# Third and fourth group's output projection as one of six steps, and an order planned in both directions

## The chip, the cores and the metric

The kernel runs on one core of one Trainium2 chip. The metric is device time in microseconds (us). TensorE is called PE below, VectorE DVE, ScalarE ACT, GpSimd POOL, and SyncE, which issues most DMAs, SP.

## The reference

Two layers are computed, for one prompt of 1024 tokens and 8 samples of 4 tokens, 1056 tokens in all, with 1024 features. Layer 0 is a Hawk block, layer 1 an HGRN2 block; a norm closes the trunk. The change lies in layer 0 and in the first two products of layer 1. Layer 0 is, cut to what matters:

```python
xn = _rmsnorm(x, g_norm)
u = xn @ w_in                                  # 1024 -> 2 x 1536
xb, gate = u[..., :1536], u[..., 1536:]
xc, new_buf = _causal_conv(xb, conv_w, conv_b, buf)      # 4 taps
r  = sigmoid(xc . w_r + b_r)                   # 16 blocks of 96
ig = sigmoid(xc . w_i + b_i)
log_a = -8 * softplus(-lam) * r
a = exp(log_a)
bterm = sqrt(-expm1(2 * log_a)) * (ig * xc)
h[t] = a[t] * h[t-1] + bterm[t]                # along the tokens
y = h * silu(gate)
return x + y @ w_out                           # 1536 -> 1024
```

## The kernel before

Features lie on the partitions, tokens along the free axis, in three chunks (c) of 352 tokens. x has 8 blocks of 128 features (k, or m for outputs); the 1536 inner features are 12 blocks in 4 groups (g) of three (j). A product in fp32 is made of three matmuls of fp32r parts (`mm3`, lines 192 to 194): high weight by high x, high by low, low by high. So every weight and every operand is split into a high part (a copy, on ACT) and a low part (a subtraction, on DVE or POOL; `subtract`, line 360). A projection of x to one block and chunk is 8 steps, 24 matmuls of 352 columns; one of a group's y to one block of x is 3 steps, 9 matmuls.

Layer 0 isn't ordered by hand. Its functions record operations in `fl`, a `Flow` (line 48): engine, an estimated duration, the call, the keys read and written, and a priority. `Flow.run` is a list scheduler: at each step it takes the engine that can start first and, among that engine's ready operations, the one of the lowest priority number, then of the earliest place in the program. The products recorded with `main=True` keep their program order on PE; the small gate products of the recurrence, the norms and the broadcasts are side work that the planner puts between them, made ready later by `SIDE`, 0.8 us. The order found is emitted as it is: each engine has its fixed queue, and an instruction that waits holds up all behind it on its engine. Layer 1 after its first six products is scheduled by the framework.

The program order of layer 0 is as follows. `begin(c, ...)` loads a chunk of x, scales and splits it, sums its squares (`squares`, L456 on ACT, L459 the adds) and takes its norm (`norm`: PE L281 sums over partitions, DVE L471, POOL's power L473, DVE L474 and L477 make a diagonal, PE L479 broadcasts it to a PSUM bank). `scaled_parts` (L484 and L485) multiplies by gain and norm and splits. Chunk 0 is split from the unnormalized x (L844, L847, L850) and its norm is applied to the products (L506, L546). `products(c)` multiplies the first six blocks of weights, group 0's gate and conv columns. `gate(g)` evaluates the gate half of a group, with ACT's tanh and a multiplication on DVE, into `sg`. `conv(g)` evaluates the other half: a 4-tap filter (L522, L525), whose result is split into X, 18 blocks that all groups use in turn (L530, L531). `lru(g)` makes the gates of the recurrence from X (PE, hg banks), rebuilds the filter's result on POOL (L601), scans (L621) and multiplies by the gate's `sg` (L629). `split_y(g)` splits the result into YH and YL (L636, L637). `out(g)` multiplies y by the output weights of the group, 8 blocks by 3 chunks of 9 matmuls, adds to x (L652), which it loads from and stores to DRAM: xT to x1a, x1a to x1b, x1b to x1c for g = 0, 1, 2. `out_last` does the same for g = 3, chunk by chunk with the weights of all eight blocks kept in X (L677, L678), adds (L691), squares on ACT, adds them on POOL, and norms for layer 1. `first1` is the first two weight blocks of layer 1.

The stages after the start stand in this order before the change:

```python
lru(0); split_y(0); gate(1); conv(1); gate(2, (0, 1)); lru(1); out(0)
gate(2, (2,)); split_y(1); conv(2); lru(2); gate(3, (0,)); out(1)
split_y(2); conv(3); gate(3, (1, 2)); lru(3); out(2); split_y(3); out_last
```

Four PSUM banks (`mm`) take the main products in turn, four (`hg`) the side products; a bank is free again when the product's evacuation has read it. Weights pass through three raw buffers (`raws`).

Of the kernel before, what the change touches and what calls it, by code (L numbers as in the profile page):

```python
# [38 lines left out]
CH = 352  # L39
# [7 lines left out]
class Flow:  # L47
# [3 lines left out]
    HOP, SIDE = 0.2, 0.8  # L51
    EARLY = {"PE": 0.0, "DVE": 0.0, "ACT": 0.0, "POOL": 0.0, "SP": 0.0}

    def __init__(self):
        self.ops = []
        self.writer = {}
        self.readers = {}
        self.main = None
        self.dma_free = 0.0
# [23 lines left out]

    def run(self):
        left = [len(o[3]) for o in self.ops]
        after = [[] for _ in self.ops]
        for i, o in enumerate(self.ops):
            for d in o[3]:
                after[d].append(i)
        ready = [0.0] * len(self.ops)  # L90
        wait = {e: [] for e in self.EARLY}
        free = dict(self.EARLY)
        for i, n in enumerate(left):
            if not n:
                wait[self.ops[i][0]].append(i)
        self.log = []
        for _ in self.ops:
            t0, e = min((max(free[e], min(ready[i] for i in q)), e) for e, q in wait.items() if q)
            q = wait[e]
            i = min((j for j in q if ready[j] <= t0), key=lambda j: (self.ops[j][4], j))  # L100
            q.remove(i)
            _, us, emit, _, _, kb, _ = self.ops[i]
            emit()
            end = free[e] = t0 + us
            if kb:
                self.dma_free = max(self.dma_free, t0 + 2.6) + kb / 250.0
                end = self.dma_free
            self.log.append((i, e, t0, end))
            for j in after[i]:
                o = self.ops[j]  # L110
                ready[j] = max(ready[j], end + (self.HOP + o[6] if o[0] != e or kb else 0.0))
                left[j] -= 1
                if not left[j]:
                    wait[o[0]].append(j)
# [12 lines left out]
def tile_trunk(ctx: ExitStack, tc: tile.TileContext, xT, prm, hc, w0, wg, wo0, w1, wo1, s_in,  # L127
# [205 lines left out]
    with ExitStack() as l0:  # L333
# [12 lines left out]
        def dma(dst, src, r=(), w=(), prio=5, kb=180, q=Q):  # L346
            fl.add("SP" if q is Q else "ACT", 0.45, lambda: q.dma_start(dst, src), r, w, prio, kb)
# [7 lines left out]
        def pool(n, emit, r, w, prio=5):  # L355
            fl.add("POOL", 0.3 + 0.0026 * n, emit, r, w, prio)
# [93 lines left out]


        def squares(k, x, xk, acc, eng=None, own=None):
# [3 lines left out]
            act(CH, lambda: S.activation(sq[:, :CH], x, AF.Square), (xk,), (sk,), 2)  # L456
# [81 lines left out]
        def gate(g, js=range(3)):  # L538
# [17 lines left out]
        def lru(g):  # L556
# [11 lines left out]
            for c in range(NCH):  # L568
# [40 lines left out]
                for j in range(3):  # L609
# [9 lines left out]
                    h, hk = ta[:, j], tak[j]  # L619
# [4 lines left out]
                    if c == 2:  # L624
                        pool(1, lambda h=h, m=m: G.tensor_copy(hst[:, m, 0:1], h[:, 319:320]), (hk,), (("hst", m),), 4)
                        pool(8, lambda h=h, m=m: G.tensor_copy(hst[:, m, 1:], h[:, 320:].rearrange("p (b j) -> p b j", j=4)[:, :, 3]),
                             (hk,), (("hst", m, 1),), 4)
                    sg, sk = sgs[g][j, c]
                    dve(CH, lambda h=h, sg=sg: V.scalar_tensor_tensor(sg, h, 0.5, sg, op0=ALU.mult, op1=ALU.mult), (hk, sk), (sk,), 3, True)  # L629

        def split_y(g):
            for c in range(NCH):
                for j in range(3):
                    sg, sk = sgs[g][j, c]
                    a, b = YH[j][:, chunk(c)], YL[j][:, chunk(c)]
                    act(CH, lambda sg=sg, a=a: S.copy(a, sg), (sk,), (("yh", j, c),), 2)  # L636
                    dve(CH, lambda sg=sg, a=a, b=b: V.tensor_tensor(b, sg, a.bitcast(F32), op=ALU.subtract),  # L637
                        (sk, ("yh", j, c)), (("yl", j, c),), 2, True)
# [4 lines left out]
        def out(g, src, dst, more, ms=range(KD)):  # L643

            own = cycle([next(xos) for _ in range(NXO)] + more)
            for m in ms:
# [19 lines left out]
        def out_last(src):  # L666

            ws = []
            for m in range(KD):
                raw, rk = next(raws)  # L670
                dma(raw[:, :384], wo0[m][:, 1152:], (), (rk,), 1, 192)
                keys = []
                for i in range(2):
                    a = (2 * m + i) * 384
                    keys.append(tuple(("X", b) for b in range(a // CH, (a + 383) // CH + 1)))
                hi, lo = (X[:, (2 * m + i) * 384:(2 * m + i + 1) * 384] for i in range(2))
                act(384, lambda hi=hi, raw=raw: S.copy(hi, raw[:, :384]), (rk,), (*keys[0], ("wl", m, 0)), 1)  # L677
                pool(384, lambda hi=hi, lo=lo, raw=raw: G.tensor_tensor(lo, raw[:, :384], hi.bitcast(F32), op=ALU.subtract),  # L678
                     (rk, ("wl", m, 0)), (*keys[1], ("wl", m, 1)), 1)
                ws.append(lambda k, hi=hi, lo=lo, m=m: (hi[:, 128 * k:128 * k + 128], lo[:, 128 * k:128 * k + 128],  # L680
                                                        (("wl", m, 0), ("wl", m, 1))))
            own = [next(xos) for _ in range(NXO)]
            spare = halves[0][:8], own + [halves[0][8]] + [halves[1][i] for i in (0, 3, 6, 1)], halves[0][:8]
            for c in range(NCH):
                acc = next(xbs)
                rows = []
                for m in range(KD):
                    ps, pk = product(ws[m], ycols(c), 1)
                    x, xk = spare[c][m]
                    dma(x, src[m][:, chunk(c)], ((3, m, c),), (xk,), 3)  # L690
                    dve(CH, lambda x=x, ps=ps: V.tensor_tensor(x, ps[:, :CH], x, op=ALU.add), (pk, xk), (xk,), 0)  # L691
                    dma(x1d[m][:, chunk(c)], x, (xk,), (("x1d", m, c),), 3)
                    squares(m, x, xk, acc)
                    rows.append((x, xk))
# [636 lines left out]
```

## Time and profile before

| | us |
|---|---|
| median of 3 runs | 1145.92 |
| lowest and highest | 1145.76, 1146.29 |
| profiled execution, its own time | 1146.4 |
| its span in the profile | 1144.6 |
| PE busy | 1111.9 |
| DVE busy | 683.0 |
| ACT busy | 487.1 |
| POOL busy | 470.0 |

The mean granted clock of PE over the span is 0.986 of full speed. In the profile an instruction is named by its source line (L192), its engine, its operation and its output and inputs by the program's names; `sg`, `xb`, `xo`, `k` and `R` are buffers that serve several purposes, and the line tells which. Windows are counted from the span's start. What an idle stretch is put down to is the operation whose completion released the waiting one. Layer 0 ends near 540 us.

### The profile page before, as it was taken

What the parts mean: (1) busy time and instruction counts of PE and PEld (TensorE: products, weight loads), DVE (VectorE), ACT (ScalarE), POOL (GpSimd) and SP (SyncE); (2) the same over time, 40 slices, a digit from 0 to 9 for tenths busy, and PEclk for the clock granted to TensorE, in tenths of its full rate; (3) what the DMA queues carried; (4) which work ended last, traced back from release to release, by engine and by line L of the source; (5) the groups of instructions that cost most, each with busy time, mean ns of one, the idle gap of its engine ahead of it and who ended that gap; (6) DMA issues with size and microseconds to landing.
All of it is one profiled execution on the core that took longest, in us unless ns stands there. A gap on an engine that the chain in (4) does not pass through costs nothing.

```text
span 1144.6 us, 24338 instructions
## 1 busy us (share of the span) xinstructions
PE 1111.9 (97%) x9688; PEld 1065.8 (93%) x9688; DVE 683.0 (60%) x1373; ACT 487.1 (43%) x1112; POOL 470.0 (41%) x491
## 2 busy tenths in 40 slices
PE   8899999999999999989999999999999999989996
PEld 7799999999999999889999999999999999979995
DVE  6988488686668857983343534443543534486426
ACT  7443767845666585552223132222223232242323
POOL 4622254434344435674143423324143423263444
PEclk9899999999999999999999999999999999999998
DMA  8201122483276238741112111121112111151204
GB/s 274 64 13 37 56 68 67 141 253 95 60 213 209 62 88 260 256 160 38 37 40 77 38 59 39 45 70 38 59 39 77 40 58 39 34 193 38 81 9 152
DMA packets 70977, 105.15 MB, mean 92 GB/s; under 512 B 9296, under 2 KB 51920, under 8 KB 70864
## 3 DMA queue, kind: packets, MB, share of 16 engines
q1 hardware_dynamic: 68704, 100.91, 28.1%
q10 hardware_dynamic: 2160, 2.69, 0.7%
q8 instruction: 76, 1.25, 0.5%
q14 instruction: 37, 0.30, 0.1%
HBM read 72.13 MB, written 26.57 MB: 86 GB/s over the span
## 4 chain that ended last, share of the span: by engine, by line
PE 89%; DVE 7%; ACT 1%; issue 1%; POOL 0%; DMA 0%; POOLq 0%; DVEq 0%; ACTq 0%
PE mm L192 26%; PE mm L194 24%; PE mm L193 24%; PE hg L986 2%; PE hg L1107 1%; PE hg L1065 1%; PE hg L586 1%; PE hg L960 1%; PE hg L1109 1%; PE hg L193 1%; PE hg L194 1%; PE hg L192 1%; DVE xl L360 1%; PE hg L1041 1%; DVE sg L484 1%
## 5 line engine op out<-in xcount | busy, mean ns | idle before, releaser
L192 PE MATMUL mm<-xh,whi 128*128 128x352 f32 x1368 | 458.6, 335 | 0.0
L193 PE MATMUL mm<-xl,whi 128*128 128x352 f32 x1368 | 443.6, 324 | 1.8 <-POOL xl L360 1.8
L194 PE MATMUL mm<-xh,wlo 128*128 128x352 f32 x1368 | 443.9, 324 | 0.1
L192 PEld LDWEIGHTS mm<-xh,whi 128*128 128x128 f32 x1368 | 258.2, 189 | 9.5 <-issue 4.2
L193 PEld LDWEIGHTS mm<-xl,whi 128*128 128x128 f32 x1368 | 258.5, 189 | 4.5 <-POOL xl L360 2.1
L194 PEld LDWEIGHTS mm<-xh,wlo 128*128 128x128 f32 x1368 | 258.0, 189 | 1.7 <-issue 1.2
L171 POOL TENSOR_TENSOR wlo<-wraw,whi 128x512 fp32r<-128x512 f32 x76 | 92.8, 1224 | 216.4 <-ACT whi L170 216.3
L360 POOL TENSOR_TENSOR wlo<-wraw,whi 128x512 fp32r<-128x512 f32 (+1 forms) x65 | 93.9, 1455 | 99.4 <-ACT whi L415 94.0
L525 DVE SCALAR_TENSOR_TENSOR k<-xb,prm_sb,k 128x352 f32<-128x352 f32 (+2 forms) x144 | 88.7, 627 | 8.3 <-ACT k L522 3.8
L170 ACT CAST whi<-wraw 128x512 fp32r<-128x512 f32 x76 | 44.0, 586 | 114.8 <-PE mm L193 95.7
L930 ACT ACTIVATE t<-mm 128x352 f32<-128x352 f32 x66 | 30.5, 461 | 110.2 <-PE mm L194 106.9
L192 PE MATMUL mm<-yh,whi 128*128 128x352 f32 x216 | 71.6, 331 | 0.5 <-DVE xo L652 0.4
L194 PE MATMUL mm<-yh,wlo 128*128 128x352 f32 x216 | 69.8, 323 | 0.0
L193 PE MATMUL mm<-yl,whi 128*128 128x352 f32 x216 | 69.8, 323 | 0.0
L1048 DVE TENSOR_TENSOR AV<-AV,Gc 128x512 f32<-128x512 f32 (+1 forms) x42 | 36.1, 860 | 42.9 <-PE hg L1041 19.7
L1120 POOL TENSOR_TENSOR rst<-rst,mhalf 128x4 f32<-128x4 f32 (+1 forms) x24 | 20.6, 861 | 90.8 <-DVE rst L1119 90.8
L601 POOL TENSOR_TENSOR k<-X 128x352 f32<-128x352 f32 x36 | 38.0, 1057 | 44.7 <-DVE R L602 40.1
L415 ACT CAST whi<-wraw 128x512 fp32r<-128x512 f32 (+1 forms) x67 | 37.3, 579 | 32.6 <-PE mm L193 17.6
L582 ACT ACTIVATE R<-hg,smalls 128x352 f32<-128x352 f32 x72 | 37.8, 553 | 11.8 <-PE hg L194 9.5
L192 PEld LDWEIGHTS mm<-yh,whi 128*128 128x128 f32 x216 | 40.7, 188 | 1.9 <-DVE xo L652 0.7
L193 PEld LDWEIGHTS mm<-yl,whi 128*128 128x128 f32 x216 | 40.7, 189 | 0.6
L945 DVE SCALAR_TENSOR_TENSOR SG<-t,mm 128x352 f32<-128x352 f32 x24 | 12.4, 519 | 48.0 <-ACT t L930 48.0
(315 smaller groups left out, 2114.2 us busy)
## 6 DMA issues: line engine op xcount, KB each, us to landing
wraw<-in_w_dram SPq DMA_DIRECT2D x105, 256.0 KB, 2.7
wraw<-in_wo_dram SPq DMA_DIRECT2D x32, 192.0 KB, 2.6
sg<-in_xT_dram SPq DMA_DIRECT2D x27, 176.0 KB, 3.8
x<-x SPq DMA_DIRECT2D x8, 528.0 KB, 4.3
si<-in_s_in_dram SPq DMA_DIRECT2D x8, 512.0 KB, 3.5
out_ss_out_dram<-si SPq DMA_DIRECT2D x8, 512.0 KB, 2.6
sg<-x1c SPq DMA_DIRECT2D x21, 176.0 KB, 4.0
x<-sg SPq DMA_DIRECT2D x21, 176.0 KB, 2.0
```

What stands on the lines that cost most here:

```text
L170: S.copy(hi, raw[:, :n])
L171: G.tensor_tensor(lo, raw[:, :n], hi.bitcast(F32), op=ALU.subtract)
L192: T.matmul(out, wh, xh, start=first, stop=False)
L193: T.matmul(out, wh, xl, start=False, stop=False)
L194: T.matmul(out, wl, xh, start=False, stop=last)
L360: emit = lambda: e.tensor_tensor(b, x, a.bitcast(F32), op=ALU.subtract)
L415: act(m, lambda hi=hi, raw=raw, m=m: S.copy(hi[:, :m], raw[:, :m]), rk, (hk,), prio)
L525: dve(u, lambda src=src, dst=dst, sh=sh, k=k: V.scalar_tensor_tensor(dst, sh(src, k), pc("cw", 12 * k + m), dst, op0=ALU.mult, op1=ALU.add ...
L582: act(CH, lambda ps=ps, R=R, i=i, j=j, hb=hb, m=m: S.activation(R[:, i, j], ps[:, :CH], AF.Tanh, bias=hb[:, m:m + 1], scale=0.5), (pk, ("s ...
L601: pool(CH, lambda x=x, a=a, b=b: G.tensor_tensor(x, a.bitcast(F32), b.bitcast(F32), op=ALU.add), (ak, bk), (xk,), 3)
L930: S.activation(t, ps[:, :CH], AF.Tanh, scale=0.5)
L1048: V.tensor_tensor(av[:, :, 1, :], av[:, :, 1, :], gv[:, :, 0:1].to_broadcast([128, nb, level]), op=ALU.mult)
```

## The change

The change has these parts.

- `out` serves groups 0 and 1 only. `out_last` multiplies the y of groups 2 and 3 at once: each of its 24 products has six steps, 18 matmuls, and adds to x1b. The loads, adds and stores of x1c go. Group 3's y lies in the places of x's first three blocks (`xcols(c)[:3]`), no longer needed by then. Its weights are 768 columns for each block instead of 384 and are loaded in 18 pieces into the places of the recurrence's gate weights (m = 4), X (m = 0 to 3), the third chunk's places of x blocks 3 to 7 (m = 5 and part of 6) and two weight buffers (the rest of 6, and 7). Blocks are taken in the order 4, 0, 1, 2, 3, 5, 6, 7, in the third chunk 6, 7, 5, 4, 0, 1, 2, 3.
- The last two gate columns of group 3 are multiplied behind the group's recurrence, chunk by chunk (`by_chunk`): the scan writes h into the gate's place, and the gate's evacuation multiplies it (`late`).
- The order of stages differs: conv(2) directly follows group 2's gates, out(0) comes behind lru(2), conv(3) and lru(3) ahead of out(1).
- In the start, chunk 0's low parts are all made on DVE (`XG` is empty), four of its squares on POOL (`MU`), the parameters are the second load of ACT's queue, and the small constants of layer 0 (`smalls`) are computed at the start, apart from layer 1's (`smalls1`).
- `Flow` plans forwards by priorities, then backwards from the end, then forwards with the backward plan's start times as priorities, eight times, and emits the shortest of the plans. `SIDE` is 1.2 us; a load's completion is a delay of its readers only.
- In `first1`, the first weight block's second chunk now comes ahead of the second block's first.

The diff, cut:

```diff
-    HOP, SIDE = 0.2, 0.8
+    HOP, SIDE = 0.2, 1.2
+    TURNS = 8
     def run(self):
+        best = got = self.plan([o[4] for o in self.ops])
+        for _ in range(self.TURNS):
+            got = self.plan(self.back(got[2]))
+            self.ends.append(got[0])
+            best = min(best, got, key=lambda g: g[0])
+        for i in best[3]:
+            self.ops[i][2]()
...
+        def by_chunk(items):
+            ws = [weights(src, 1024) for src, _ in items]
+            for c in range(NCH):
+                for w, (_, evac) in zip(ws, items):
+                    evac(c, *product(w, xcols(c)))
+                    yield
...
+            if mult:
+                pool(CH, lambda: G.tensor_tensor(sq[:, :CH], x, x, op=ALU.mult), (xk,), (sk,), 2)
+            else:
+                act(CH, lambda: S.activation(sq[:, :CH], x, AF.Square), (xk,), (sk,), 2)
...
+                    if late:
+                        t, tk = next(ts)
+                        act(CH, lambda: S.activation(t, ps[:, :CH], AF.Tanh, scale=0.5), (pk,), (tk,), 0)
+                        dve(CH, lambda: V.scalar_tensor_tensor(t, t, 1.0, ps[:, :CH], op0=ALU.add, op1=ALU.mult), (pk, tk), (tk,), 0)
+                        dve(CH, lambda: V.scalar_tensor_tensor(sg, sg, 0.5, t, op0=ALU.mult, op1=ALU.mult), (tk, sk), (sk,), 1, True)
+                        return
...
         def out_last(src):
-            ws = []
-            for m in range(KD):
-                raw, rk = next(raws)
-                dma(raw[:, :384], wo0[m][:, 1152:], (), (rk,), 1, 192)
+            def load(m, k, n, hi, hks, lo, lks, kept=()):
+                raw, rk = next(raws)
+                u = 128 * n
+                a, b = ("wl", m, 0, k), ("wl", m, 1, k)
+                dma(raw[:, :u], wo0[m][:, 768 + 128 * k:768 + 128 * k + u], (), (rk,), 1, u / 2)
+                act(u, lambda: S.copy(hi, raw[:, :u]), (rk,), (*hks, a), 1)
+                pool(u, lambda: G.tensor_tensor(lo, raw[:, :u], hi.bitcast(F32), op=ALU.subtract), (rk, a), (*lks, b), 1)
...
             for c in range(NCH):
-                for m in range(KD):
-                    ps, pk = product(ws[m], ycols(c), 1)
-                    dma(x, src[m][:, chunk(c)], ((3, m, c),), (xk,), 3)
+                for i, m in enumerate(ms[c]):
+                    ps, pk = product(blocks[m].get, ycols(c) + xcols(c)[:3], 1)
+                    dma(x, src[m][:, chunk(c)], ((2, m, c),), (xk,), 3)
...
-        VI, XG = (0, 2), (1, 3, 5)
+        VI, XG, MU = (0, 2), (), [(0, k) for k in range(1, 8, 2)]
...
-        run(project0(gate(2, (0, 1))))
+        gates, rest = project0(gate(2)), out(0, xT, x1a)
+        run(islice(gates, 6))
         lru(1)
-        run(out(0, xT, x1a, halves[0][6:]))
-        run(project0(gate(2, (2,))))
-        split_y(1)
+        run(gates)
         run(project0(conv(2)))
         lru(2)
-        run(project0(gate(3, (0,))))
-        run(out(1, x1a, x1b, halves[1][3:]))
+        run(rest)
+        split_y(1)
+        run(project0(gate(3,(0,))))
+        rest = out(1, x1a, x1b)
+        run(project0(conv(3)))
+        lru(3)
+        run(rest)
+        run(by_chunk(gate(3, (1, 2), True)))
         split_y(2)
-        run(project0(conv(3)))
-        run(project0(gate(3, (1, 2))))
-        lru(3)
-        run(out(2, x1b, x1c, halves[0]))
         split_y(3)
-        out_last(x1c)
+        out_last(x1b)
```

More of the change, by code (lines that the diff above doesn't have):

```diff
@@ L1 @@
 from contextlib import ExitStack, nullcontext
-from itertools import cycle
+from itertools import cycle, islice
 import numpy as np
@@ L47 @@
 class Flow:
-    HOP, SIDE = 0.2, 0.8
-    EARLY = {"PE": 0.0, "DVE": 0.0, "ACT": 0.0, "POOL": 0.0, "SP": 0.0}
+    HOP, SIDE = 0.2, 1.2
+    ENGINES = ("PE", "DVE", "ACT", "POOL", "SP")
+    TURNS = 8
+    ends = []
     def __init__(self):
@@ new lines, in back @@
+    def back(self, key):
+        n = len(self.ops)
+        left = [len(a) for a in self.after]
+        ready = [0.0] * n
+        wait = {e: [] for e in self.ENGINES}
+        free = dict.fromkeys(self.ENGINES, 0.0)
+        for i in range(n):
+            if not left[i]:
+                wait[self.ops[i][0]].append(i)
+        starts = [0.0] * n
+        for _ in range(n):
+            t0, e = min((max(free[e], min(ready[i] for i in q)), e) for e, q in wait.items() if q)
+            q = wait[e]
+            i = max((j for j in q if ready[j] <= t0), key=lambda j: (key[j], j))
+            q.remove(i)
+            _, us, _, deps, _, kb, _ = self.ops[i]
+            free[e] = t0 + max(us, kb / 250.0)
+            starts[i] = -t0 - us
+            for j in deps:
+                ready[j] = max(ready[j], t0 + us + self.lag(j, i))
+                left[j] -= 1
+                if not left[j]:
+                    wait[self.ops[j][0]].append(j)
+        return starts
@@ L84, in run @@
     def run(self):
-        left = [len(o[3]) for o in self.ops]
-        after = [[] for _ in self.ops]
+        self.after = [[] for _ in self.ops]
         for i, o in enumerate(self.ops):
             for d in o[3]:
[L89 to L114, printed above, removed]
+                self.after[d].append(i)
@@ L536, in tile_trunk, with gate @@
         sgs = [{} for _ in range(4)]
-        def gate(g, js=range(3)):
+        def gate(g, js=range(3), late=False):
             items = []
@@ L741, in smalls @@
             ttv(t1, pv("lam"), nl, ALU.min)
-            seq(("ACT", lambda: S.activation(e, t1, AF.Exp)))
+            seq((("sm",),), 0.5, ("ACT", lambda: S.activation(e, t1, AF.Exp)))
             v(V.tensor_scalar, t1, e, 2.0, None, op0=ALU.add)
@@ L874, in tile_trunk @@
         products(2)
-        smalls()
+        smalls1()
         masks()
-        x1b, x1c = ([nc.dram_tensor(f"x1{n}_{m}", (128, TOK), F32, kind="Internal").ap() for m in range(KD)] for n in "bc")
+        x1b = [nc.dram_tensor(f"x1b_{m}", (128, TOK), F32, kind="Internal").ap() for m in range(KD)]
         lru(0)
```

138 lines of the change are left out of this document (99 added, 39 removed).

## The prediction

> **What bounds the kernel now.** I read the page's head first, for the engine that is never idle, then the table of windows, for where it is idle after all, then the list of TensorE's waits in those places.
>
> ```profile
> span 1144.6 us, 24338 instructions
> ...
> PE 1111.9 (97%) x9688; PEld 1065.8 (93%) x9688; DVE 683.0 (60%) x1373; ACT 487.1 (43%) x1112; POOL 470.0 (41%) x491
> ```
>
> TensorE (PE) is the bound: 97% busy. A change of order that leaves its matmuls alone can win only where it waits or runs at a low clock. The windows (length; busy time and count of PE, PEld, DVE, ACT, POOL; granted clock; DMA share; GB/s) show that place by place:
>
> ```profile
> 0.00:20.00 20.00, 18.84 (x113) 18.27 (x114) 12.71 (x22) 15.30 (x31) 6.77 (x14) 1.00 0.94 321
> 20.00:40.00 20.00, 14.55 (x74) 13.18 (x73) 17.84 (x34) 12.44 (x27) 14.36 (x14) 0.83 0.29 91
> 40.00:60.00 20.00, 16.54 (x89) 15.01 (x89) 19.06 (x34) 8.87 (x19) 12.99 (x14) 0.91 0.23 74
> 60.00:460.00 400.00, 399.50 (x2442) 393.10 (x2441) 293.90 (x550) 250.95 (x494) 160.91 (x181) 1.00 0.39 117
> 460.00:480.00 20.00, 17.41 (x101) 16.61 (x100) 19.03 (x30) 10.99 (x21) 13.99 (x12) 0.95 0.92 293
> 480.00:500.00 20.00, 18.74 (x114) 18.23 (x114) 17.93 (x37) 9.17 (x19) 15.11 (x19) 0.96 0.48 155
> 500.00:520.00 20.00, 17.25 (x98) 16.61 (x96) 12.95 (x26) 8.62 (x17) 13.31 (x17) 0.91 0.37 121
> 520.00:540.00 20.00, 18.15 (x103) 17.78 (x102) 8.73 (x17) 7.20 (x16) 10.46 (x11) 0.91 0.14 47
> 540.00:560.00 20.00, 20.00 (x126) 20.00 (x126) 1.04 (x2) 4.52 (x9) 3.87 (x3) 1.00 0.10 33
> ```
>
> The last row is the yardstick: 126 matmuls in 20 us, 0.159 us from start to start. Against it, 20 to 60 us lacks 252 - 163 = 89 matmuls, 14.1 us, and 460 to 540 us, the last projection, lacks 504 - 416 = 88, 14.0 us. The 400 us between lack 0.5 us of busy time, and the rest of layer 1 isn't touched. So no reordering of layer 0 can win more than about 28.6 us. DVE, nearly full in both lossy places, is 73% busy in the middle. The waits (total, times, longest, us) name who is late, in 0 to 60 us:
>
> ```profile
> PE hg L479 <- DVE k L477: 3.4, 2, 2.6
> PE hg L281 <- DVE R L459: 2.0, 1, 2.0
> PE hg L281 <- POOL R L459: 1.7, 1, 1.7
> PE mm L194 <- POOL yl L360: 1.4, 1, 1.4
> ```
>
> and in 440 to 536.5 us:
>
> ```profile
> PE mm L192 <- DVE sg L691: 6.6, 4, 2.8
> PE mm L193 <- POOL xl L360: 1.8, 1, 1.8
> ```
>
> These sum to 8.5 and 8.4 us; the other 5.6 us in each place is clock. Three matmuls from the timeline show it (start, length), the first after a wait of 2.61 us, the second still in its wake, the third past it:
>
> ```profile
> 29.94 1.54 PE L479 MATMUL hg<-k,ones 128*128 128x352 f32 x2 [2.61 <-DVE k L477]
> ...
> 32.15 0.49 PE L192 MATMUL mm<-xh,yh 128*128 128x352 f32 x1
> ...
> 35.63 0.33 PE L192 MATMUL mm<-xh,yh 128*128 128x352 f32 x1
> ```
>
> The Trainium skill ("TensorE: Matmul & The Clock Gate", Part 1) has the clock fall only after an idle window of some 3.4 us, so that shorter waits would cost themselves alone. The trace disagrees: a wait of 2.61 us is followed by lengths of 0.49 us. By the page the tail below would be worth at most its 8.4 us; by the windows 14.0. I go by the windows.
>
> **The change, part by part.**
>
> *One six-step projection instead of two of three (tail).* The 24 products of 9 matmuls of the third group, and their 24 adds, loads and stores, go; the last 24 products have 18 matmuls. PE's count is the same: in the queues of both kernels, which stand fixed once each is built ("the order after" below), PE's row 3003 is the first of layer 1's scheduled part, and from there the rows are the same. What alters is the pace of DVE's work per product:
>
> ```profile
> L360 DVE TENSOR_TENSOR xl<-sg,xh 128x352 fp32r<-128x352 f32 x15 | 12.8, 889 | 0.4 <-ACT xh L485 0.4
> L484 DVE SCALAR_TENSOR_TENSOR sg<-sg,prm_sb,hg 128x352 f32<-128x352 f32 x21 | 11.1, 574 | 2.8 <-PE hg L479 2.7
> L691 DVE TENSOR_TENSOR sg<-mm,sg 128x352 f32<-128x352 f32 x21 | 10.6, 514 | 2.5 <-PE mm L194 2.3 <-DMA sg<-x1c 0.2
> ```
>
> One chunk asks of DVE 8 adds (4.1 us), 8 scalings (4.6), 6 subtractions (5.3): 14.0 us. PE's chunk is now 72 x 0.159 = 11.4 us, so DVE sets the pace, and PE waits for banks. After, it is 144 x 0.159 = 22.9 us, and DVE has 9 us to spare in each. The wait for the third chunk's low part (1.8 us, xl of L360) shrinks too: in the order after, 42 matmuls stand between that chunk's norm broadcast and its first use, 6.7 us, against 30 now. POOL is next in line:
>
> ```profile
> L459 POOL TENSOR_TENSOR xb<-xb,k 128x352 f32<-128x352 f32 x21 | 22.7, 1082 | 4.6 <-ACT k L456 3.6
> L678 POOL TENSOR_TENSOR X<-wraw,X 128x384 fp32r<-128x384 f32 x8 | 9.9, 1241 | 15.2 <-ACT X L677 9.6 <-DMA x1c<-xo 5.6
> ```
>
> The weights are twice as many: 18 pieces (10 of 384 columns, 7 of 256, 1 of 512, 6144 columns) for 8; at 1241 ns for 384 that is 19.9 us of POOL, plus 8 adds of 1.08 us in the first chunk, 28.5 us. The last block is wanted 22.9 us (late gates, six products) + 7 x 2.9 us = 43 us after those gates begin. Walking POOL's and SP's queues in the order after, with the pieces for m = 5 to 7 held back until the gates' last chunk has read the places they go into, I get the pieces ready 1.5 to 3 us before use at the closest, m = 6 and 7. SP carries 46 instructions fewer in all, and what stands behind a held-back piece on it is loads of x wanted 5 us later. I take 13 us of the 14.0; ends 8 (the listed waits go, a late piece brings the clock down again) and 14.
>
> *Adds, loads and stores of the third group gone.* 24 x 0.51 us of DVE, 24 loads and stores: priced at 0, since PE stands still 0.5 us in the 400 us where they lie. They are slack for the next part.
>
> *Gates behind the recurrence.* Two gate columns of group 3 are multiplied after the scan: two DVE operations and one ACT per chunk as before. Between chunk 0's gates and its first use stand four products, 15 us, against some 3 us of work each. Priced at 0; without that cover each late chunk costs its 3 us.
>
> *Stages moved, planner run both ways (middle).* conv(2) follows conv(1) by 9 products, 35 us, instead of about 70; both write the same X. In the order after, the last of lru(1)'s matmuls that read X stands 54 rows behind conv(2)'s first, so the two interleave. Nothing in the trace prices this. DVE's 293.9 us in the 400, less 12 us of adds, leave over 100 us idle, so I charge 1 us; ends 0 and 8, the latter two waits like the largest of the start, 2.6 us with about 1.5 of low clock each.
>
> *Start.* The activation table is loaded ahead of the first wait, all eight low parts of chunk 0 are on DVE (three leave POOL), four squares go to POOL, the parameters come first, with some 28 tiny operations on DVE before its first evacuation, and one more half weight is loaded ahead of x's last three blocks (256 KB at 321 GB/s, 0.8 us).
>
> ```profile
> 3.16 1.28 ACT L844 ACT_TABLE_LOAD   x1 [3.16 <-DMA sg<-in_xT_dram]
> ...
> L459 DVE TENSOR_TENSOR xb<-xb,xo 128x352 f32<-128x352 f32 x7 | 5.6, 799 | 0.3
> L850 DVE SCALAR_TENSOR_TENSOR xl<-sg,g,xh 128x352 fp32r<-128x352 f32 x5 | 3.5, 706 | 5.0 <-ACT xh L844 5.0
> ...
> 84.97 0.17 DVE L731 TENSOR_TENSOR smalls<-smalls 128x12 f32<-128x12 f32 x1
> 85.18 1.30 DVE L731 TENSOR_SCALAR smalls<-smalls 128x12 f32<-128x12 f32 x1
> ...
> L459 POOL TENSOR_TENSOR R<-R,xo 128x352 f32<-128x352 f32 x7 | 7.2, 1024 | 0.2
> ```
>
> DVE takes on 3 x 0.71 + 28 x 0.21 (0.17 and the step between two) = 8.0 us, some with the odd stretch to 1.3 us seen here. Against that stand 5.0 us in which it waited for ACT, now filled, and squares no longer queued behind ACT's casts. Following PE's queue: the sum of chunk 1's squares ends at about 24 us as now, the broadcast of the first norm follows at about 28, that of the second behind the fifth product's first matmuls instead of stalling PE at 29.94, and the fifth product starts at 31 to 34 us against 35.63. The second chunk's first product starts at 40 to 44.5 against
>
> ```profile
> 48.26 0.64 PE L192 MATMUL mm<-xh,X 128*128 128x352 f32 x1
> ```
>
> since by POOL's queue in the order after, its weight parts for these products are through by 22 to 24 us and the third chunk's squares by about 35, when PE comes to them. That is 4 to 8 us; I take 5.5. Ends: 11 (nearly all of 14.1) and -2 (every tiny operation at 0.4 us, 5 us more, and POOL's squares 4 x 1.02 us in DVE's way, 4.1, eat it all and more).
>
> The Trainium skill ("SBUF — State Buffer", "SBUF: two separate sides") says that DVE with two inputs and GpSimd exclude each other for a whole instruction. Here adds with two inputs take 799 ns beside POOL and 514 ns with one input from PSUM, which agrees in kind. By that rule the squares moved to POOL cost DVE up to 4.1 us and the start is worth 1.4; that is inside the second rival.
>
> *Sum:* 13 + 5.5 - 1 = 17.5 us. The profiled execution took 1146.4 us, 1.8 around its span; the median shown is 1145.92, 0.5 below it. 1145.9 - 17.5 = **1128.4 us**.
>
> **The rivals.**
>
> 1. *Start worth nothing.* For it: DVE is 89 to 95% busy from 20 to 60 us and gets 8 us more. Against: what PE waited for on POOL stands earlier in POOL's queue, and the broadcast of the second chunk's norm stands 24 rows later on PE. 1145.9 - 13 + 1 = 1133.9 us.
> 2. *Weight pieces late in the tail.* m = 6 or 7 is late; each wait of 2 us costs 3.5 with its clock. For it: margins of 1.5 to 3 us, three raw buffers for 18 pieces. Against: POOL has 28.5 us to do in 43. Tail 7: 1145.9 - 7 - 5.5 + 1 = 1134.4 us.
> 3. *Nearly everything goes.* 14 + 10, no charge: 1121.9 us. For it: the order after shows no other engine near its limit in the tail. Against: warm-up and first norms can't all be hidden.
> 4. *Slower: conv(2) waits for X.* If lru(1) is a whole chunk behind when conv(2)'s parts want its X, the evacuations stop, four banks fill, and PE stands still at about 200 us. A chunk is 293.9 us over about 11 chunks, 26.7 us of DVE, so 1128.4 + 26.7 - 1 = 1154 us. It decides from 18.5 us on, two thirds of a chunk. For it: half the distance. Against: DVE's 100 us of idle time, and the interleaved order.
> 5. *The change doesn't do what it says:* the merged products stand in the order of instructions, so only the planner's gain can be absent, which is rival 1.
>
> **How the numbers follow.** Forecast 0.48 (its own range 1123 to 1133), rival 1 0.18, rival 2 0.10, rival 3 0.08, rival 4 0.13, the parts cancelling to within 0.2% (2.3 us, about what a measurement of this kernel can tell from no change) 0.03. Faster 0.84, same 0.03, slower 0.13. The range takes in rivals 1 to 3 and part gains of the start and tail: from 1117, where all 28.6 us would be gone, to 1142, where the tail's 8 is left with a start of -2 and 2 of stalls; outside it lie rival 4 and no change, 0.16.
>
> **What would show it.** Tail: waits of PE for the projection's adds gone, a window of 126 matmuls each from the first of the 18-matmul products on, granted clock 1.00; wrong if PE waits there for POOL's weight parts. Start: 20 to 60 us with more than 200 matmuls instead of 163; wrong if PE waits for DVE's first evacuation beyond 34 us. Middle: 60 to 460 us with under 2 us idle; any PE wait for DVE's X or POOL's L601 would be rival 4. The prediction fails if a wait over 5 us stands between 60 and 460 us.

## The result and the profile after

| | before | after |
|---|---|---|
| median, us | 1145.84 (4 runs) | 1128.64 (4 runs) |
| lowest and highest, us | 1144.89, 1146.29 | 1127.48, 1128.90 |
| span of the profiled execution, us | 1144.6 | 1126.9 |

The ratio is 0.9849, with a 95% interval of 0.9832 to 0.9866. 1128.4 us was forecast. The number is right; the profile shows that two of its three terms are not, and the experiments show that only about half of the largest, the tail, is the merged projection's work. The planner gave the other half.

The head of the page after:

```profile
span 1126.9 us, 24255 instructions
...
PE 1103.7 (98%) x9688; PEld 1059.9 (94%) x9688; DVE 691.9 (61%) x1352; ACT 487.4 (43%) x1107; POOL 471.7 (42%) x494
```

PE is busy 8.2 us less with the same 9688 matmuls: busy time at a low clock has gone as well as waits. Three windows are enough for layer 0 (length; busy time and count of PE, PEld, DVE, ACT, POOL; clock; DMA share; GB/s). Before:

```profile
0.00:60.00 60.00, 49.94 (x272) 46.46 (x273) 49.61 (x88) 36.62 (x76) 34.12 (x41) 0.91 0.49 162
60.00:440.00 380.00, 379.50 (x2318) 373.10 (x2317) 279.39 (x525) 238.88 (x470) 151.00 (x174) 1.00 0.37 109
440.00:540.00 100.00, 91.55 (x534) 89.24 (x533) 73.14 (x134) 48.04 (x95) 62.78 (x64) 0.95 0.56 177
```

After:

```profile
0.00:60.00 60.00, 49.08 (x272) 45.97 (x273) 49.98 (x109) 30.63 (x65) 32.72 (x42) 0.91 0.50 161
60.00:440.00 380.00, 380.00 (x2325) 374.18 (x2325) 321.66 (x538) 263.64 (x512) 171.64 (x192) 1.00 0.37 111
440.00:540.00 100.00, 100.00 (x626) 99.36 (x625) 40.03 (x80) 32.56 (x67) 48.00 (x50) 1.00 0.29 92
```

The tail, 440 to 540 us, is full: 626 matmuls at a clock of 1.00 against 534, 92 more, 14.7 us at 0.16 each. The middle has no wait left and 7 matmuls more, 1.1 us. The start has not moved: 272 matmuls in 60 us in both. It only loses its time elsewhere, in its first 20 us, as the same stretches as in the prediction show:

```profile
0.00:20.00 20.00, 14.37 (x75) 12.76 (x76) 14.30 (x27) 12.46 (x26) 9.89 (x16) 0.90 0.90 296
20.00:40.00 20.00, 14.72 (x85) 13.93 (x83) 18.89 (x47) 9.19 (x21) 13.27 (x13) 0.93 0.40 127
40.00:60.00 20.00, 20.00 (x114) 19.29 (x115) 16.79 (x37) 8.98 (x20) 9.56 (x14) 0.92 0.21 61
```

From 20 to 60 us there are 199 matmuls instead of 163, but up to 20 us only 75 instead of 113. The largest waits of PE after, 0 to 60 us:

```profile
PE mm L241 <- DVE xl L952: 4.6, 5, 1.9
PE mm L240 <- DVE sg L612: 3.8, 1, 3.8
PE hg L538 <- DVE k L536: 1.5, 1, 1.5
```

(L952 makes chunk 0's low parts, L850 before; L612 is the first evacuation, L546 before; L536 was L477.) Layer 1 begins its first transposition at these times, before and after:

```profile
563.30 1.03 PE L960 MATMUL hg<-ident,R 128*128 128x128 f32 x8
```

```profile
547.36 1.03 PE L1063 MATMUL hg<-ident,R 128*128 128x128 f32 x8
```

So layer 0 gave 15.9 of the 17.7 us between the spans. From here to the end of the span it is 581.3 us before and 579.5 after, for the same order of instructions; over all fourteen profiles this stretch lies between 578.3 and 581.3 us, so the other 1.8 us are scatter between executions, and the profile before has the longest of the fourteen.

### The profile page after: what moved, and what is told of

Read it like the earlier page. It is cut to its first block, busy times and chain, and to the rows that moved or that the text cites. A ratio compares the mean times of both kernels' runs of the same rounds, so it can differ in the third digit from the quotient of the medians.

```text
span 1126.9 us, 24255 instructions
## 1 busy us (share of the span) xinstructions
PE 1103.7 (98%) x9688; PEld 1059.9 (94%) x9688; DVE 691.9 (61%) x1352; ACT 487.4 (43%) x1107; POOL 471.7 (42%) x494
## 4 chain that ended last, share of the span: by engine, by line
PE 94%; DVE 4%; issue 1%; DMA 0%; ACT 0%; POOL 0%; ACTq 0%; POOLq 0%; DVEq 0%
PE mm L240 27%; PE mm L241 25%; PE mm L242 25%; PE hg L1089 2%; PE hg L1168 1%; PE hg L1210 1%; PE hg L652 1%; PE hg L1063 1%; PE hg L1212 1%; PE hg L240 1%; PE hg L241 1%; PE hg L242 1%; DVE smalls L825 1%; PE hg L1144 1%; PE hg L1234 1%
## 5 line engine op out<-in xcount | busy, mean ns | idle before, releaser
L241 PE MATMUL mm<-xl,whi 128*128 128x352 f32 x1383 | 449.8, 325 | 4.6 <-DVE xl L952 4.6
L242 PE MATMUL mm<-xh,wlo 128*128 128x352 f32 x1383 | 448.7, 324 | 0.0
L408 POOL TENSOR_TENSOR wlo<-wraw,whi 128x512 fp32r<-128x512 f32 (+1 forms) x57 | 83.3, 1469 | 68.0 <-ACT whi L463 63.1
L667 POOL TENSOR_TENSOR k<-X 128x352 f32<-128x352 f32 x36 | 41.6, 1157 | 69.9 <-DVE R L668 64.3
L240 PE MATMUL mm<-yh,whi 128*128 128x352 f32 x153 | 51.0, 333 | 0.0
L241 PE MATMUL mm<-yl,whi 128*128 128x352 f32 x153 | 49.5, 324 | 0.0
L242 PE MATMUL mm<-yh,wlo 128*128 128x352 f32 x153 | 49.5, 324 | 0.0
L648 ACT ACTIVATE R<-hg,smalls 128x352 f32<-128x352 f32 x72 | 38.5, 554 | 15.9 <-DVE R L688 8.6
L1048 DVE SCALAR_TENSOR_TENSOR SG<-t,mm 128x352 f32<-128x352 f32 x24 | 12.4, 518 | 47.5 <-ACT t L1033 47.5
L1093 DVE COPY_PREDICATED attnd<-mask,hg 128x256 f32<-128x256 uint8 x40 | 17.7, 443 | 38.8 <-PE hg L1126 22.1
L1041 POOL TENSOR_SCALAR G<-t,smalls 128x352 f32<-128x352 f32 x21 | 25.5, 1215 | 33.0 <-ACT t L1033 33.0
L463 ACT CAST whi<-wraw 128x512 fp32r<-128x512 f32 (+1 forms) x59 | 33.8, 588 | 12.1 <-PE mm L241 7.0
```

What stands on the lines that cost most here:

```text
L240: T.matmul(out, wh, xh, start=first, stop=False)
L241: T.matmul(out, wh, xl, start=False, stop=False)
L242: T.matmul(out, wl, xh, start=False, stop=last)
L408: emit = lambda: e.tensor_tensor(b, x, a.bitcast(F32), op=ALU.subtract)
L463: act(m, lambda hi=hi, raw=raw, m=m: S.copy(hi[:, :m], raw[:, :m]), rk, (hk,), prio)
L648: act(CH, lambda ps=ps, R=R, i=i, j=j, hb=hb, m=m: S.activation(R[:, i, j], ps[:, :CH], AF.Tanh, bias=hb[:, m:m + 1], scale=0.5), (pk, ("s ...
```

## Experiments: planner or merged projection

The forecast's theory was that the merged projection frees the tail, because it halves the pace at which DVE's work per product is asked for. The rival: the planner frees it. The first kernel keeps everything but the merge.

```diff
         split_y(2)
+        run(out(2, x1b, x1c))  # 9 matmuls, behind the late gates
         split_y(3)
...
-        out_last(x1b)        # 18 matmuls a product
+        out_last(x1c)        # 9 matmuls, three weight blocks kept in X
```

> The changed kernel with the third and fourth group's projections apart again, 24 products of 9 matmuls with their loads, adds and stores of x1c, then 24 of 9 with weights of three steps kept in X; planner, order of stages, late gates and start stay. Theory (DVE's 14 us per chunk against PE's 11.4 set the tail's pace, and merging lifts that): the 14 us of the tail come back, 1140 to 1145 us, with PE waiting for the last projection's adds. Rival (the planner's two directions freed the tail): within 2 us of the changed kernel's 1128.6.

1137.12 us, ratio 0.9921 (0.9902 to 0.9940): 8.5 us come back, not 14, so the time lies between the two expectations. PE waits in the tail for the last projection's adds again (4.1 us in two waits), as the theory has it. The second kernel is the one before with the new planner, its code cut to what matters.

```diff
-    HOP, SIDE = 0.2, 0.8
+    HOP, SIDE = 0.2, 1.2
     def run(self):
-        ...                  # one pass, by priority
+        best = got = self.plan([o[4] for o in self.ops])
+        for _ in range(self.TURNS):
+            got = self.plan(self.back(got[2]))
```

> The kernel before with the changed kernel's planner alone (forwards and backwards in turn, SIDE 1.2), its program otherwise untouched. Theory (DVE's pace per product sets the tail): the tail stays as it is, 1143 to 1147 us. Rival (the planner gave the gain): 1128 to 1133 us.

1133.43 us, ratio 0.9892 (0.9870 to 0.9914). The theory falls: 12.4 us are gained without any merge. They don't all lie in the tail, though, as the windows below show. Is it the backward pass, or the new constants (`SIDE` and the reckoning of loads)? The same with `TURNS = 0`:

> The kernel before with the new planner, but forwards alone (no turns): SIDE 1.2 and the other reckoning of loads stay. Theory (the backward plan's due times, not the constants, gave the 12.3 us): 1143 to 1147 us. Rival (the constants gave it): 1132 to 1136 us.

1146.59 us, ratio 1.0002 (0.9990 to 1.0014): the backward pass. And the other corner, the changed program with the old planner:

```diff
-    HOP, SIDE = 0.2, 1.2
+    HOP, SIDE = 0.2, 0.8
-        best = got = self.plan([o[4] for o in self.ops])
-        for _ in range(self.TURNS):
-            got = self.plan(self.back(got[2]))
+        ...                  # one pass, by priority
```

> The changed kernel's program with the planner of before (forwards alone, SIDE 0.8). The planner alone brought 12.3 us and taking the merge away cost 8.5. Theory (the two are different cures of one loss, the tail, so they don't add): the merged tail stays dense without the new planner, at least 75 of 80 us busy from 460 to 540 us, and the rest is the start's, 1130 to 1137 us. Rival (the merge needs the backward plan to have its 18 weight pieces in time): over 1139 us, with PE waiting for POOL's weight parts in the tail.

1147.64 us, ratio 1.0007 (0.9998 to 1.0017): without the backward pass the changed program as a whole gains nothing. Neither expectation holds in whole: the rival's time came, but PE waits for POOL's weight parts in the tail for 1.8 us only. The windows from 440 to 540 us of the four kernels, in the order told:

```profile
440.00:540.00 100.00, 94.22 (x575) 92.43 (x574) 50.26 (x99) 35.21 (x73) 53.82 (x58) 0.98 0.56 181
```

```profile
440.00:540.00 100.00, 94.21 (x580) 92.07 (x579) 62.12 (x122) 46.10 (x92) 60.41 (x63) 1.00 0.52 170
```

```profile
440.00:540.00 100.00, 91.48 (x543) 89.14 (x542) 74.94 (x133) 48.87 (x94) 56.34 (x62) 0.97 0.55 176
```

```profile
440.00:540.00 100.00, 92.37 (x557) 89.57 (x556) 50.76 (x99) 37.09 (x78) 53.89 (x63) 0.98 0.31 101
```

Against 626, the matmuls lacking are 92 before, 83 with the new constants alone, 46 with the backward pass, 51 without the merge, 69 with the merge and the old planner. So in the tail the planner alone is worth 46 matmuls, 7.3 us; the rest of its 12.4 us is 26 matmuls, 4.2 us, in the start (298 in 60 us, shown below) and 6 in the middle. The merge, with the new planner, is worth 51 matmuls in the tail, 8.1 us. Together that is about the 92.

Has the planner taken work off DVE in the tail? These windows end at a fixed time, and where layer 0 is shorter they take in some of layer 1. Counted back from layer 1's first transposition, at 563.30 us before, 550.75 with the planner alone, 555.70 without the merge, 566.64 with the old planner and 547.36 in the changed kernel, the same 100 us are, with the planner alone, without the merge and in the changed kernel:

```profile
427.45:527.45 100.00, 94.21 (x580) 92.07 (x579) 72.19 (x138) 49.31 (x97) 63.49 (x66) 1.00 0.61 197
```

```profile
432.40:532.40 100.00, 94.22 (x574) 92.43 (x573) 56.47 (x113) 35.52 (x74) 56.71 (x61) 0.98 0.63 203
```

```profile
424.06:524.06 100.00, 100.00 (x625) 99.36 (x624) 55.30 (x104) 36.78 (x77) 58.26 (x62) 1.00 0.37 115
```

DVE is busy 73.1 us before and 72.2 with the planner alone: the planner took no work off it there. The last scan, the end of the fourth group's recurrence, before, with the planner alone, with the old planner and in the changed kernel, shows the same:

```profile
481.12 1.12 DVE L621 TENSOR_TENSOR_SCAN R<-a,R,R 128x352 f32<-128x352 f32 x1
```

```profile
471.19 1.70 DVE L669 TENSOR_TENSOR_SCAN R<-a,R,R 128x352 f32<-128x352 f32 x1
```

```profile
448.42 1.36 DVE L640 TENSOR_TENSOR_SCAN sg<-a,sg,R 128x352 f32<-128x352 f32 x1
```

```profile
435.38 1.37 DVE L688 TENSOR_TENSOR_SCAN R<-a,R,R 128x352 f32<-128x352 f32 x1
```

It begins 82.2 us ahead of the first transposition before, 79.6 with the planner alone, 118.2 with the new order of stages and the old planner, 112.0 with both. So it is the order of stages that brings the recurrence forward, and that alone doesn't fill the tail: without the merge DVE has 56.5 us to do instead of 72.2, and the tail lacks 51 matmuls against 46. What the planner alone altered in the tail is 2.6 us less of waits (5.8 against 8.4) and a granted clock of 1.00 instead of 0.95. Why its order does that stays open, and so does what the order of stages is worth by itself, or the merge in the kernel before: neither was run.

With the old planner the merged tail is all but dense from 460 us on, but the last projection's fourth product waits 4.5 us for the evacuation of a late gate (L559), the case without cover of which the forecast spoke. The tail still has 23 matmuls more than before. The gain goes elsewhere: the start lacks 27 more (245 in 60 us against 272), and the middle 19 (2299 against 2318):

```profile
445.78 0.43 PE L192 MATMUL mm<-yh,X 128*128 128x352 f32 x1 [4.48 <-DVE k L559]
```

```profile
460.00:540.00 80.00, 77.82 (x480) 76.15 (x481) 37.17 (x77) 27.50 (x56) 38.55 (x43) 1.00 0.30 98
```

## Experiments: does DVE set the tail's pace

One more DVE operation behind each of the 24 last adds, which leaves x as it is, in both kernels.

```diff
                     dve(CH, lambda x=x, ps=ps: V.tensor_tensor(x, ps[:, :CH], x, op=ALU.add), (pk, xk), (xk,), 0)
+                    dve(CH, lambda x=x: V.tensor_tensor(x, x, x, op=ALU.max), (xk,), (xk,), 0)
```

> The changed kernel with one more DVE operation of 352 columns behind each of the 24 last adds (the maximum of x with itself, in place, 0.5 to 0.8 us each, 4 to 6.4 us per chunk). Theory (after, DVE has 9 us to spare per chunk of 22.9): 0 to 1 us more. Rival (the tail has become balanced to its limit): 5 us or more.

> The same 24 operations in the kernel before. Theory (DVE sets the tail's pace there): nearly all of 24 times 0.5 to 0.8 us shows, 10 to 18 us more, 1156 to 1164 us. Rival (the tail waits for latencies between engines, not for DVE's throughput): under 5 us more.

After: 1128.86 us, ratio 0.9847 (0.9829 to 0.9866), no change against the changed kernel. Before: 1153.25 us, ratio 1.0067 (1.0045 to 1.0088), 7.5 us more. The window after, with the added operations (53.8 us of DVE instead of 40.0), and the groups of the added operation and the window in the kernel before:

```profile
440.00:540.00 100.00, 99.99 (x624) 99.06 (x623) 53.83 (x103) 31.55 (x66) 48.81 (x51) 1.00 0.29 94
```

```profile
L692 DVE TENSOR_TENSOR sg<-sg 128x352 f32<-128x352 f32 x21 | 14.4, 688 | 0.7
...
L692 DVE TENSOR_TENSOR xo<-xo 128x352 f32<-128x352 f32 x3 | 1.8, 592 | 0.1
```

```profile
440.00:540.00 100.00, 87.94 (x492) 83.50 (x490) 86.97 (x157) 46.32 (x90) 59.21 (x60) 0.91 0.54 175
```

Of 16.2 us of added work, less than half shows (42 matmuls fewer in the window, 6.7 us). So DVE does set the tail's pace before and not after, but for a part of it only: 10 to 18 us was too much, and the rival's 5 too little. (This profile is of the slowest run, 1155.61 us; its start, which the edit doesn't touch, is 20 matmuls short of the 272 as well.) After, DVE has time to spare in the tail for at least the 13.8 us more that it did there; that it has 9 us in every chunk was not tried to the end.

## Experiments: the start

Why did the start not gain? DVE's queue after, in the stretch ahead of the first evacuation (start, length), and POOL's operation beside it:

```profile
28.66 0.91 DVE L825 TENSOR_SCALAR smalls<-smalls 128x12 f32<-128x12 f32 x1
...
34.46 1.28 DVE L825 TENSOR_SCALAR smalls<-smalls 128x12 f32<-128x12 f32 x1
...
39.44 1.37 DVE L612 TENSOR_TENSOR sg<-mm,R 128x352 f32<-128x352 f32 x3
```

```profile
34.42 1.30 POOL L408 TENSOR_TENSOR yl<-wraw,yh 128x512 fp32r<-128x512 f32 x1
```

Between 28.7 and 39.4 us DVE does little but the small constants. They go back behind the first products in the program, at a lower priority:

```diff
-                seq((("sm",),), 0.5, ("DVE", lambda: f(*a, **k)))
+                seq((("sm",),), 6, ("DVE", lambda: f(*a, **k)))
...
-        smalls()
         begin(0, 0, 2)
...
+        smalls()
         smalls1()
         masks()
```

> The changed kernel with the small constants of layer 0 computed behind the first products again, at the old priority. The changed kernel's start came out as long as that of before, with PE waiting 3.8 us for DVE's first evacuation, in front of which some 25 tiny operations take 28.7 to 39.3 us. Theory (these hold the evacuation back): the wait of 3.8 us, 1.5 us of the broadcast before it and their low clock go, 1122 to 1125 us. Rival (the sums of squares and the norms behind POOL set that time, the tiny operations only fill): 1127.5 to 1129.5 us.

1123.61 us, ratio 0.9788 (0.9774 to 0.9803), beside 1148.62 us for the kernel before on that chip; the next three ran beside it, and are best compared by their ratios. The theory holds in the main: the wait of 3.8 us is down to 1.3, and that of 1.5 to 0.2. Each of these edits makes the planner plan anew, so that more moves than the edited lines: here 15 of the constants still stand ahead of the first evacuation, which begins at 36.29 us instead of 39.44. Next, the low parts and squares alone as before the change:

```diff
-        VI, XG, MU = (0, 2), (), [(0, k) for k in range(1, 8, 2)]
+        VI, XG, MU = (0, 2), (1, 3, 5), []
```

> The changed kernel with three of chunk 0's low parts on POOL again and its four squares on ACT again; small constants early. Theory (eight low parts on one engine hold back the first product: 4.6 us of waits and low clock): the first product's waits go, but the evacuation's wait for DVE stays and takes up part of it: 1125 to 1128 us. Rival (all of it is taken up by the later wait, because DVE as a whole is the bound of the first 40 us): 1128 to 1129.5 us.

1130.00 us, ratio 0.9841 (0.9827 to 0.9856): nothing, as the rival's time had it, but not for its reason. PE no longer waits for the first evacuation. The planner now puts 11 of the constants between 11.5 and 17.5 us, ahead of two low parts, and PE waits there:

```profile
18.17 0.66 PE L241 MATMUL mm<-xl,whi 128*128 128x352 f32 x1 [3.57 <-DVE xl L952]
```

So the waits of the first product didn't go, and this run can't tell what the low parts and squares alone cost. Both edits, and both with the parameters' load back on SP's queue:

> Both: small constants late, three low parts on POOL and all squares on ACT. Theory (two costs that hide the start's gain): 1118 to 1122 us. Rival (POOL or ACT is the next bound at once): no better than the better of the two alone.

> As the last, and the parameters' load where it was before, on the other queue behind the first weights: the start as before the change but for the planner and the table's load. Theory (the parameters' place costs nothing of note once the constants are late): within 1 us of the last. Rival (its bytes or its place on ACT's queue delay the first weights): 1 to 3 us faster than the last.

1125.76 us, ratio 0.9805 (0.9790 to 0.9819), and 1124.27 us, 0.9795 (0.9779 to 0.9812). Both together are no better than the constants alone, as the rival has it; 1118 to 1122 us wasn't reached. The place of the parameters can't be told from nothing by these intervals. Last, constants late and the squares back on ACT, but all low parts left on DVE:

```diff
-        VI, XG, MU = (0, 2), (), [(0, k) for k in range(1, 8, 2)]
+        VI, XG, MU = (0, 2), (), []
```

> The changed kernel with the small constants late (1123.6 us, beside a slower kernel before) and all squares on ACT again, all low parts still on DVE. Theory (POOL's four squares hold DVE up, 4 us at most): 1 to 4 us faster than that, ratio to before 0.975 to 0.978. Rival (ACT is as short of time as DVE and the squares are better off on POOL): 1 to 3 us slower, ratio 0.980 to 0.982.

1120.88 us, ratio 0.9771 (0.9757 to 0.9786): within the first expectation, though the interval overlaps that of the constants alone. It is the fastest of all, 25.6 us under the kernel before on that chip. That it is the squares isn't shown, since the plan differs too: only 7 constants are left ahead of the first evacuation, which begins at 31.35 us. The kernel with both edits differs from this one only in its three low parts on POOL; its ratio of 0.9805 is clear of 0.9771, so here the low parts are better off on DVE. With the parameters late:

> The last kernel (small constants late, squares on ACT, all low parts on DVE: 1120.9 us, ratio to before 0.977) with the parameters loaded where they were before the change, behind the first weights on SP's queue. Theory (74 KB at some 300 GB/s, 0.25 us, and one place in a queue): within 1 us of it, ratio 0.976 to 0.978. Rival (the first weights come earlier by the place they get back on ACT's queue, and the first product with them): 1 to 2 us faster, 0.975 or less.

1122.12 us, ratio 0.9784 (0.9768 to 0.9801): no gain, so the rival falls. The theory's 0.978 is just missed, within the interval. Against the ratio of 0.9795 with three low parts on POOL this can't be told apart. The windows from 0 to 60 us: planner alone, constants late, low parts and squares as before, squares on ACT.

```profile
0.00:60.00 60.00, 51.67 (x298) 48.59 (x299) 47.46 (x85) 35.57 (x74) 32.62 (x40) 0.97 0.51 162
```

```profile
0.00:60.00 60.00, 52.96 (x301) 50.58 (x302) 52.21 (x101) 32.35 (x68) 33.03 (x43) 0.94 0.51 162
```

```profile
0.00:60.00 60.00, 49.94 (x271) 45.62 (x272) 51.01 (x112) 34.22 (x73) 32.21 (x41) 0.89 0.50 161
```

```profile
0.00:60.00 60.00, 52.98 (x312) 49.74 (x313) 49.79 (x116) 33.88 (x72) 29.86 (x39) 0.97 0.50 162
```

The new planner is worth 26 matmuls, 4.2 us, in the old start (298 against 272), and the start's other edits take all of it away again (272). With the constants late there are 301, and with the squares on ACT as well 312; with both edits 295, and 300 with late parameters. The last kernel has only 285, but its profile is of its slowest run, 1123.45 us.

## Why the prediction was right, and where it was not

*The sum, -17.5, came to -17.7 between the spans, by cancellation.* Start: 5.5 us forecast, 0 measured. Tail: 13 forecast, 14.7 measured. Middle: 1 us charged, 1.1 gained; no wait stands between 60 and 440 us. 1.8 us of the difference between the spans is scatter in layer 1. That the number was met so closely is luck.

*Tail: the size was right, the cause was half of it.* The step that failed is crediting the merge with 13 of the 14.0 us that the tail lacked. The prediction's own pace accounts for less: 14.0 us of DVE's work against 11.4 of PE's per chunk is 2.6 us, and three chunks of it are 7.8. The merge measured 8.5 us, so this mechanism stands, at its own size. For the rest the prediction took all waits and all low clock of the tail for the merge's to lift. "DVE, nearly full in both lossy places" hid the difference: its rows from 460 to 540 us add up to 58.6 us of DVE in 80, 73%, as in the middle, and the last 20 us lack 23 matmuls with DVE busy for 8.7. The rest is the planner's, which alone is worth 7.3 us in the tail. The prediction priced it in the middle, as a risk, and not as a gain. The spare time of DVE that it counted on is there: 13.8 us more of DVE's work in the tail cost nothing.

*Start: the condition of rival 1 came true.* Its time, 1133.9 us, did not, since the tail and the middle gave more than it took and layer 1 scattered the same way. The start's gain was forecast for 20 to 60 us and came there, 36 matmuls or 5.7 us. The step that failed is putting nothing on the first 20 us, where 38 matmuls, 6.0 us, were lost. There PE waits five times in the first product for low parts that DVE makes between adds, the last time at 18.58 us. The two DVE operations before it, and PE:

```profile
15.81 2.22 DVE L518 TENSOR_TENSOR xb<-xb,xo 128x352 f32<-128x352 f32 x2
17.95 0.58 DVE L952 SCALAR_TENSOR_TENSOR xl<-sg,g,xh 128x352 fp32r<-128x352 f32 x1
```

```profile
18.58 0.66 PE L241 MATMUL mm<-xl,whi 128*128 128x352 f32 x1 [1.41 <-DVE xl L952]
...
22.84 0.32 PE L240 MATMUL mm<-xh,whi 128*128 128x352 f32 x1
```

PE comes back to full clock only at 22.8 us. "5.0 us in which it waited for ACT, now filled" were filled, but the adds came ahead of low parts that PE was waiting for. Eight low parts on DVE don't cost this by themselves: the fastest kernel has them too, and 101 matmuls in its first 20 us. The sum of the second chunk's squares was put at 24 us "as now"; DVE's last three adds for it run from 26.95 to 28.74, and PE takes the sum at 29.23:

```profile
26.95 1.79 DVE L518 TENSOR_TENSOR R<-R,xo 128x352 f32<-128x352 f32 x3
```

```profile
29.23 0.67 PE L329 MATMUL hg<-ones,R 128*128 128x1 f32 x6
```

And the fifth product, put at 31 to 34 us, began at 40.00:

```profile
40.00 0.66 PE L240 MATMUL mm<-xh,yh 128*128 128x352 f32 x1 [3.79 <-DVE sg L612]
```

The small constants were priced as 28 x 0.21 us, 5.9; in the first 60 us 32 of them took 10.2. Each long one like that at 34.46 us adds a whole microsecond, and they stand on the path itself, between two norms and the first evacuation. The lower end, -2, covered this; the value taken did not. (Where the text on the rule of the shared port says "inside the second rival", it is the first that is meant.)

*Rival 2*, late weight pieces: no wait for them in the tail after. *Rival 3*, nearly everything goes: so it was in the tail, not in the start. *Rival 4*, conv(2) waiting for X: no wait there.

*The listed waits against the windows* (8.4 or 14.0 us): the windows were right, the tail gave 14.7.

## What to carry to other kernels

Hold a term of the sum against its own mechanism: a stage lacked 14 us, the pace named for it explained 7.8, and the rest belonged to something else. Before crediting a restructured stage, run the new order alone and the new structure alone, and read each by windows: here the planner without the structure gave 12.4 us, of which 7.3 lay in the tail, and the structure is worth 8.5 where the planner is new. Where a stage moves in time, count its windows from its end: at fixed times DVE seemed to have 11 us less to do in the tail with the planner alone, and counted from the end it had 1 us less. Ask what a change takes from the stretch in front of the one that it is to help. A chain of tiny operations placed "in idle time" ahead of the first evacuation was the dearest part of the start that was found: making it late gave 5 us more (7 by the ratios), and with the squares back on ACT came the fastest kernel, 1120.88 us.

## What the hardware showed that was not expected

A DVE operation on 128x12 elements, 0.17 us elsewhere, took 1.28 us beginning at 34.46 and ended at 35.74; POOL's subtraction beside it ran from 34.42 to 35.72. The small operation lasted as long as the large one on the other engine. The Trainium skill ("SBUF — State Buffer", "SBUF: two separate sides") has DVE and GpSimd exclude each other for a whole instruction, where DVE's runs in a mode that takes two ports or has two inputs in SBUF. This row agrees that one waits for the other to end; the operation held up has one tensor as input, and no run here shows in which mode it ran.

Low clock doesn't follow from a wait's length alone. In the tail before, each of these waits was followed by some 3 us of matmuls of 0.49 or 0.50 us:

```profile
477.79 0.43 PE L192 MATMUL mm<-yh,X 128*128 128x352 f32 x1 [2.34 <-DVE sg L691]
...
505.19 0.43 PE L192 MATMUL mm<-yh,X 128*128 128x352 f32 x1 [2.75 <-DVE sg L691]
...
528.53 0.43 PE L193 MATMUL mm<-xl,whi 128*128 128x352 f32 x1 [1.85 <-POOL xl L360]
```

With the planner alone, a wait of nearly the same length left the clock at 1.00 throughout the tail:

```profile
475.25 0.43 PE L240 MATMUL mm<-yh,X 128*128 128x352 f32 x1 [2.58 <-DVE sg L739]
```

In the tail before, the granted clock falls at 478.19, 505.50 and 529.39 us, whole multiples of 3.41 us apart, and each time it stays at half for 3.41 us. The stretches of 3.41 us just ahead of the three low ones, and the first low one, are:

```profile
474.78:478.19 3.41, 1.07 (x7) 0.77 (x6) 3.38 (x6) 0.74 (x2) 3.41 (x4) 1.00 0.87 281
478.19:481.60 3.41, 3.41 (x14) 3.41 (x13) 3.37 (x6) 2.39 (x6) 3.15 (x4) 0.50 0.76 240
502.09:505.50 3.41, 0.66 (x5) 0.37 (x4) 3.41 (x9) 2.44 (x6) 0.86 (x1) 1.00 0.57 189
525.98:529.39 3.41, 1.56 (x10) 1.27 (x9) 2.50 (x4) 1.96 (x6) 3.41 (x4) 1.00 0.00 0
```

PE is idle for 69, 81 and 54% of the stretch ahead of a low one. With the planner alone, the same steps, counted on from the clock's last change before, at 26.90 us, cut the wait of 2.58 us in two, and neither part leaves PE idle for more than 41% of a stretch:

```profile
470.64:474.05 3.41, 2.03 (x13) 1.73 (x11) 3.37 (x4) 1.78 (x4) 3.31 (x4) 1.00 0.52 152
474.05:477.46 3.41, 2.21 (x13) 2.21 (x14) 2.02 (x5) 1.32 (x3) 2.65 (x3) 1.00 0.59 177
```

So for these four waits it is where the wait lies among the steps, and not its length, that goes with the clock; part of what the planner alone gained in the tail may be this chance. It isn't a rule for every place: in the start before, the stretch from 20.81 to 24.22 us is idle for 54% and the clock stays up behind it, and the one from 24.22 to 27.63 for 38% and the clock falls. The Trainium skill ("TensorE: Matmul & The Clock Gate", Part 1) speaks of an idle window of some 3.4 us; no wait here was that long where the clock fell in the tail of before.
